# A two-layer hybrid transformer block on one core: the last layer's z modulations left out, and the low parts of the last branch and the output projection moved to VectorE

## The chip, the cores and the metric

The kernel runs on one core of a Trainium2 chip. The metric is the device time of one execution in microseconds (us); the medians given are over repeated executions. The engines are named as in the profile: PE is TensorE (matmuls; PEld its weight loads), DVE is VectorE, ACT is ScalarE, POOL is GpSimd, SP is SyncE, which here issues most DMAs.

## The reference

Two token streams, x (512 tokens) and z (256 context tokens) of width 1024, go through two layers. The modulations of a layer are six vectors of 1024 for x and six for z. In the last layer (`need_ctx` false) z is only read by the token mixers: its outputs, and so all of its modulations past the first two, are used by nobody.

```python
def hybrid_layer(x, z, c, c_ctx, p, rope_ret, rope_mla, need_ctx):
    mod_x = jax.nn.silu(c) @ p['w_ada'] + p['b_ada']
    mod_z = jax.nn.silu(c_ctx) @ p['w_ada'] + p['b_ada']
    sh1x, sc1x, g1x, sh2x, sc2x, g2x = [m[:, None, :] for m in jnp.split(mod_x, 6, axis=-1)]
    sh1z, sc1z, g1z, sh2z, sc2z, g2z = jnp.split(mod_z, 6, axis=-1)
    hx = x * (1.0 + sc1x) + sh1x
    hz = z * (1.0 + sc1z) + sh1z
    mix_x, mix_z = token_mixers(hx, hz, p, rope_ret, rope_mla, need_ctx)
    x = layer_norm(DEEPNORM_ALPHA * x + g1x * mix_x, p['ln_gain'][0], p['ln_bias'][0])
    x = layer_norm(DEEPNORM_ALPHA * x + g2x * sq_relu_mlp(x * (1.0 + sc2x) + sh2x, p),
                   p['ln_gain'][1], p['ln_bias'][1])
    if need_ctx:
        ...
    else:
        z = None
    return x, z
```

`token_mixers` sums three gated branches, `sigmoid(gate) * (y @ w_branch)`, and multiplies the sum by `w_out` (the output projection). `sq_relu_mlp` is `square(relu(h @ w_ff1)) @ w_ff2`.

## The kernel before

**Products in three matmuls.** All activations lie feature-major, 128 features by tokens. A float32 operand is kept as a pair: a high part (`hi_of`, ScalarE, a rounding copy to fp32r) and a low part (`lo_of`, source minus high part). Line 386 is every such subtraction; it runs on VectorE unless another engine is given. A product is three matmuls (lines 432 to 434): weight high by operand high, weight high by operand low, weight low by operand high. So line 433 waits for the operand's low part and line 434 for the weight's.

**Weights.** `weight` loads a 128x1024 block (tile `wraw`, three buffers), makes the high part on ScalarE and the low part in two halves: the first `w_dve` columns on VectorE, the others on GpSimd. `W_DVE` is 512. The pair goes to one of three buffers `wsp`, which TensorE frees; three blocks of the last layer's output projection (`KEPT`, tile `w`) have buffers of their own.

**Modulations.** Each layer has 48 units of 128 features. A unit is one 512 KB load and, per stream, one 128x1024 multiply-and-reduce on VectorE (line 500, tile `cond`), then a small adjustment of both results (line 506). Units 0 to 15 are shift and scale of the first half-layer. Layer 0's units from 16 on and all 48 of layer 1 are made during layer 0 by `modulations`, a generator that the rest of the program advances at set rates (`later.step`) and empties after round 6 of the MLP (`later.rest`). After the first 24 its loads have one buffer only, `graw`: the next load starts when the unit's last reduction is done.

**Branches.** `branch` computes for each of 8 feature tiles f, and for each stream, a matmul group into a PSUM bank (`pd`, three buffers; `pst` for two early ones), then VectorE multiplies it by the gate (line 1492, tile `ms`, gate tile `gl`) and the product is added to the total (line 1493, tile `t`). In the last branch (`final`) the addition is on VectorE and the total is split into `op`, the operand of the output projection: high part on ScalarE, low part on GpSimd. A bank is free again after line 1492. Layer 0 has both streams (512 and 256 columns), layer 1 only x.

**Output projection and MLP.** Per tile f of the projection, one weight block and 24 matmuls, then line 1719 (residual) and the sums for the layer norm (lines 1507 to 1513). The MLP has 8 rounds j: `ff1` (relu on ScalarE, square on VectorE, line 1756, tile `rl`, split into `op`), then `ff2`, whose banks VectorE drains into the accumulators (line 1770; in round 6 followed by line 1772, which uses a gate modulation; in round 7 line 1774). Rounds 0 and 7 go stream by stream, rounds 1 to 6 take both.

**Order.** A scheduler orders each engine's instructions when the program is built, by the order of the code and its own estimates; `keep_in_program_order` pins the reductions of `modulations` among themselves. Each engine then runs its list strictly in order.

Of the kernel before, what the change touches and what calls it, by code (L numbers as in the profile page):

```python
# [16 lines left out]
DEPTH = 2  # L17
# [21 lines left out]
W_DVE = 512  # L39

KEPT = (2, 3, 4)
# [271 lines left out]
def block_kernel(ctx, tc, xT, zT, cond, wu, sp, bias, tab, out):  # L313
# [65 lines left out]
    act, dve, pool, pe, sync = nc.scalar, nc.vector, nc.gpsimd, nc.tensor, nc.sync  # L379
# [19 lines left out]
    for l in range(DEPTH):  # L399
        t = const.tile([128, SP_N], F32, name=f"sp{l}")  # L400
# [16 lines left out]
    def weight(*key, own=False, spare=False, w_dve=W_DVE):  # L417
        raw = load(*key, spare=spare)
        if own:
            w = (dbl("w"), dbl("w"))  # L420
        else:
            t = wsp.tile([128, 2, 1024], F32, tag="wsp", name=nm("wsp"))
            w = (t[:, 0], t[:, 1])
        hi_of(w[0], raw)
        for eng, cols in ((dve, slice(0, w_dve)), (pool, slice(w_dve, 1024))):
            if cols.start < cols.stop:
                lo_of(w[1][:, cols], raw[:, cols], w[0][:, cols], eng)
        return w
# [26 lines left out]
    mods = [const.tile([128, 48, 2], F32, name=f"mod{l}") for l in range(DEPTH)]  # L455
# [34 lines left out]
    def modulation(l, c, raw, cs, pinned=False, shared=()):  # L490

        for t in shared:
            h = dbl("prod")
            pool.tensor_tensor(h, raw, cs[t], op=ALU.mult)
            act.activation(h, h, AF.Copy, scale=0.5, accum_out=mods[l][:, c, t : t + 1])
            dve.tensor_scalar(mods[l][:, c, t : t + 1], mods[l][:, c, t : t + 1], spt[l][:, SP_BADA + c : SP_BADA + c + 1], 0.0, op0=ALU.add, op1=ALU.add)
        for t in [t for t in range(2) if t not in shared]:
            i = dve.tensor_tensor_reduce(cs[2], raw, cs[t], 0.5, spt[l][:, SP_BADA + c : SP_BADA + c + 1], ALU.mult, ALU.add, mods[l][:, c, t : t + 1])  # L500
            if pinned:
                tc.keep_in_program_order(i)
        m = mods[l][:, c, :]
        add, mul = MOD_ADJUST[c // 8]
        if (add, mul) != (0, 1):
            dve.tensor_scalar(m, m, float(add), float(mul), op0=ALU.add, op1=ALU.mult)
# [70 lines left out]
    def split_into(pair, src, eng=None):  # L577
        hi_of(pair[0], src)
        lo_of(pair[1], src, pair[0], eng)
# [870 lines left out]
    def branch(l, b, sizes, ops, gates, total, final, midway=None):  # L1450

        fresh = not total
        if fresh:
            total.extend(new_tiles(n, KT) for n in sizes)
        tiles = [(f, g, n) for f in range(KT) for g, n in enumerate(sizes)]

        def fetch(f, g, n):
            t = ft("gl")[:, :n]  # L1460
            sync.dma_start(t, gates[b, f][g])
            return t

        ahead = fetch(*tiles[0])
        early = []
        ops = [[o[g] for o in ops] for g in range(len(sizes))]
        for i, (f, g, n) in enumerate(tiles):
            if midway and i == len(tiles) // 2:
                midway()
            if f % 2 == 0 and g == 0:  # L1470
                w = weight(l, "br", b, f // 2)
                if final and f == 0:

                    for ff, gg, nn in tiles[: 2 * len(sizes)]:
                        ps = (bank_d() if gg == 0 else bank_t())[:, :nn]
                        fm(ps, w, 512 * ff, ops[gg], range(3), 4)
                        early.append(ps)
            t = ahead
            if i + 1 < len(tiles):
                ahead = fetch(*tiles[i + 1])  # L1480
            if early:
                ps = early.pop(0)
                fm(ps, w, 512 * (f % 2), ops[g], [3], 4)
            else:
                ps = bank_d()[:, :n]
                fm(ps, w, 512 * (f % 2), ops[g], range(4), 4)
            a = total[g][f]
            if fresh:
                dve.scalar_tensor_tensor(a, t, 1.0, ps, ALU.add, ALU.mult)
            else:  # L1490
                s = sgl("ms")[:, :n]
                dve.scalar_tensor_tensor(s, t, 1.0, ps, ALU.add, ALU.mult)  # L1492
                (dve if final else pool).tensor_tensor(a, a, s, op=ALU.add)
                if final:
                    split_into(final[g][f], a, pool)
            yield cost(12 * n)


# [126 lines left out]
    for l in range(DEPTH):  # L1625
        need = l < DEPTH - 1
# [74 lines left out]
        def out_weight(f):  # L1701

            if f in kept:
                return kept.pop(f)
            w = weight(l, "out", f, own=not need and r == 0 and f in KEPT)
            if not need and r == 0 and f in KEPT:
                kept[f] = w
            return w

        later.until(1 + 8)  # L1710
        for r, (b, cols) in enumerate(rounds):
# [20 lines left out]
            for f in range(f0, KT):  # L1732
                w = out_weight(f)
# [11 lines left out]
        for j in range(8):  # L1745
            apart = j in (0, 7)
            for rnd in [[r] for r in rounds] if apart else [[(b, slice(0, n)) for b, (_, n) in enumerate(bufs)]]:
# [3 lines left out]
                for i in range(4):  # L1751
                    w = weight(l, "ff1", j, i)
                    for g, ps in enumerate(fm_groups(w, 0, hs, KT)):
                        t = sgl("rl")[:, : ns[g]]
# [22 lines left out]
                for i in range(4):  # L1777
                    w = weight(l, "ff2", j, i)
# [90 lines left out]
```

## Time and profile before

| | |
|---|---|
| median of 3 runs | 2669.43 us (2669.32 to 2672.81) |
| profiled execution | 2672.0 us, span 2670.0 us |
| PE busy | 2524.7 us, 95% of the span |
| DVE busy | 1801.6 us, 67% |
| ACT busy | 1157.5 us, 43% |
| POOL busy | 1048.8 us, 39% |
| mean granted clock of TensorE | 0.978 |

The profiled execution is 2.0 us longer than its span, and 2.6 us above the median. A busy share is an average over stages with different limits; for the change, the stages to look at are the last branch and output projection of layer 0 (about 870 to 960 us), rounds 1 to 7 of layer 0's MLP (about 1060 to 1540 us), and the last branch and output projection of layer 1 (about 2200 to 2290 us).

### The profile page before, as it was taken

How to read it: one execution, taken by the hardware profiler on the slowest of the kernel's cores; microseconds unless marked ns; L12 is line 12 of the kernel's file. 1: busy time of each engine (PE TensorE's matmuls, PEld its weight loads, DVE VectorE, ACT ScalarE, POOL GpSimd, SP SyncE). 2: the span in 40 equal slices, each digit the busy share in tenths (PEclk: the TensorE clock that was granted, in tenths of full speed). 3: DMA queues.
4: the chain of work that ended last, by engine and by line, in shares of the span. 5: the costliest groups of instructions: out<-in, count | busy, mean ns of one | idle time of the engine just before them, and what ended most of it. 6: DMA issues, size and time to landing. Idle time of an engine off the chain costs nothing. (4 is left out here: it accounts for less than half of the span.)

```text
span 2670.0 us, 40740 instructions
## 1 busy us (share of the span) xinstructions
PE 2524.7 (95%) x15218; PEld 2241.1 (84%) x15218; DVE 1801.6 (67%) x3326; ACT 1157.5 (43%) x2176; POOL 1048.8 (39%) x816
## 2 busy tenths in 40 slices
PE   6999999997999898999999989999999899999997
PEld 4899998987888787888888878888888788888887
DVE  8565556676978894767777775566568758734357
ACT  4555545563323345222222345555556434632225
POOL 6312113345335655222222452222334557743334
PEclk8999999999999999999999999999999999999999
DMA  6222223423665543344444423332342356433333
GB/s 237 72 87 83 72 85 95 141 78 98 237 205 153 191 127 103 111 133 125 134 134 122 133 83 114 96 96 88 117 149 91 103 185 206 127 111 95 98 100 119
DMA packets 143001, 329.48 MB, mean 123 GB/s; under 512 B 16978, under 2 KB 54738, under 8 KB 142804
## 3 DMA queue, kind: packets, MB, share of 16 engines
q1 hardware_dynamic: 132436, 311.15, 37.7%
q10 hardware_dynamic: 10368, 15.73, 1.6%
q8 instruction: 120, 1.97, 0.3%
q14 instruction: 77, 0.63, 0.1%
HBM read 288.27 MB, written 36.45 MB: 122 GB/s over the span
## 5 line engine op out<-in xcount | busy, mean ns | idle before, releaser
L432 PE MATMUL pd<-op,wsp 128*128 128x512 f32 (+1 forms) x3080 | 1074.8, 350 | 38.6 <-DVE ms L1492 8.4
L433 PE MATMUL pd<-op,wsp 128*128 128x512 f32 (+1 forms) x3080 | 1073.0, 348 | 14.6 <-DVE op L386 8.4
L434 PE MATMUL pd<-op,wsp 128*128 128x512 f32 (+1 forms) x3080 | 1069.3, 347 | 7.1 <-DVE wsp L386 7.1
L386 POOL TENSOR_TENSOR wsp<-wraw,wsp 128x512 fp32r<-128x512 f32 x317 | 522.3, 1650 | 988.3 <-ACT wsp L383 874.3
L432 PEld LDWEIGHTS pd<-op,wsp 128*128 128x128 f32 x3080 | 588.6, 192 | 115.8 <-ACT op L588 10.0
L433 PEld LDWEIGHTS pd<-op,wsp 128*128 128x128 f32 x3080 | 590.2, 192 | 87.7 <-DVE op L386 12.3
L434 PEld LDWEIGHTS pd<-op,wsp 128*128 128x128 f32 x3080 | 589.3, 191 | 80.1 <-DVE wsp L386 9.4
L383 ACT ACTIVATE wsp<-wraw 128x1024 fp32r<-128x1024 f32 x319 | 336.2, 1055 | 391.5 <-PE pd L434 271.1
L386 DVE TENSOR_TENSOR wsp<-wraw,wsp 128x512 fp32r<-128x512 f32 (+1 forms) x319 | 283.3, 889 | 190.7 <-ACT wsp L383 184.7
L647 PE MATMUL pd<-wsp,op 128*128 128x256 f32 x704 | 203.1, 289 | 2.5 <-DVE pr L757 2.0
L649 PE MATMUL pd<-wsp,op 128*128 128x256 f32 x704 | 201.3, 286 | 0.2 <-POOL wsp L386 0.2
L648 PE MATMUL pd<-wsp,op 128*128 128x256 f32 x704 | 201.1, 286 | 0.0
L500 DVE CUSTOM_DVE_ANT_0 cond<-graw,cond,sp 128x1024 bf16<-128x1024 f32 x112 | 167.5, 1495 | 43.3 <-DMA graw<-wu 42.8
L1756 DVE TENSOR_TENSOR rl<-rl 128x256 f32<-128x256 f32 (+1 forms) x104 | 68.6, 659 | 138.9 <-ACT rl L1755 138.6
L386 DVE TENSOR_TENSOR pt<-pst,pt 128x512 fp32r<-128x512 f32 (+1 forms) x208 | 121.3, 602 | 48.2 <-ACT pt L383 46.4
L647 PEld LDWEIGHTS pd<-wsp,op 128*128 128x128 f32 x704 | 137.1, 195 | 3.6 <-issue 2.8
L649 PEld LDWEIGHTS pd<-wsp,op 128*128 128x128 f32 x704 | 136.6, 194 | 0.8 <-POOL wsp L386 0.4
L648 PEld LDWEIGHTS pd<-wsp,op 128*128 128x128 f32 x704 | 137.0, 195 | 0.1
L1770 DVE TENSOR_TENSOR t<-pd,t 128x512 f32<-128x512 f32 (+1 forms) x132 | 80.4, 613 | 77.6 <-PE pd L434 77.4
L1755 ACT ACTIVATE rl<-pd 128x256 f32<-128x256 f32 (+1 forms) x104 | 51.6, 496 | 174.3 <-PE pd L434 174.2
L616 PE MATMUL pso<-pt,t 128*128 128x256 f32 x704 | 115.3, 293 | 10.7 <-DVE ntx L623 4.0
L383 ACT ACTIVATE pt<-pst 128x512 fp32r<-128x512 f32 (+1 forms) x208 | 104.8, 529 | 46.4 <-PE pst L599 39.8
(284 smaller groups left out, 3925.8 us busy)
## 6 DMA issues: line engine op xcount, KB each, us to landing
wraw<-wu SPq DMA_DIRECT2D x327, 512.0 KB, 3.7
graw<-wu SPq DMA_DIRECT2D x56, 512.0 KB, 3.7
ada<-wu SPq DMA_DIRECT2D x40, 512.0 KB, 5.7
gg<-gate ACTq DMA_DIRECT2D x48, 256.0 KB, 2.0
gl<-gg SPq DMA_DIRECT2D x48, 256.0 KB, 3.6
zbias<-bias SPq DMA_DIRECT2D x64, 128.0 KB, 2.3
t<-vd SPq DMA_DIRECT2D x28, 256.0 KB, 5.4
gd<-gt SPq DMA_DIRECT2D x40, 128.0 KB, 2.4
```

What stands on the lines that cost most here:

```text
L383: act.activation(R(dst), src, AF.Copy, scale=scale)
L386: (eng or dve).tensor_tensor(R(dst), src, hi, op=ALU.subtract)
L432: pe.matmul(ps, R(a[0]), R(b[0]), start=start, stop=False)
L433: pe.matmul(ps, R(a[0]), R(b[1]), start=False, stop=False)
L434: pe.matmul(ps, R(a[1]), R(b[0]), start=False, stop=stop)
L500: i = dve.tensor_tensor_reduce(cs[2], raw, cs[t], 0.5, spt[l][:, SP_BADA + c : SP_BADA + c + 1], ALU.mult, ALU.add, mods[l][:, c, t : t + 1])
L616: pe.matmul(o, R(vts[k]), R(pts[k]), start=k == 0, stop=k == n - 1)
L647: pe.matmul(ps, R(a[0]), R(w[0][:, o : o + 256]), start=k == 0, stop=False)
L648: pe.matmul(ps, R(a[1]), R(w[0][:, o : o + 256]), start=False, stop=False)
L649: pe.matmul(ps, R(a[0]), R(w[1][:, o : o + 256]), start=False, stop=k == nk - 1)
L1756: dve.tensor_tensor(t, t, t, op=ALU.mult)
L1770: dve.tensor_tensor(a, ps, a, op=ALU.add)
```

## The change

1. In the last layer, units 16 to 47 make only the modulation of x; the reduction for z is left out, and the adjustment of line 506 covers one column. The loads are as they were. These 32 units are the last that `modulations` makes.
2. The weights of the last branch and of the output projection, in both layers, take their low part whole on VectorE (`w_dve` 1024): one subtraction of 1024 columns in place of one of 512 there and one of 512 on GpSimd.
3. The low part of the last branch's total is made on VectorE, not on GpSimd.

```diff
-        for t in [t for t in range(2) if t not in shared]:
+        for t in [t for t in range(2) if t not in shared and (t == 0 or c < 16 or l < DEPTH - 1)]:
             i = dve.tensor_tensor_reduce(cs[2], raw, cs[t], 0.5, spt[l][:, SP_BADA + c : SP_BADA + c + 1], ALU.mult, ALU.add, mods[l][:, c, t : t + 1])
             if pinned:
                 tc.keep_in_program_order(i)
-        m = mods[l][:, c, :]
+        m = mods[l][:, c, : 2 if c < 16 or l < DEPTH - 1 else 1]
...
-                w = weight(l, "br", b, f // 2)
+                w = weight(l, "br", b, f // 2, w_dve=1024 if final else W_DVE)
...
                 if final:
-                    split_into(final[g][f], a, pool)
+                    split_into(final[g][f], a)
...
-            w = weight(l, "out", f, own=not need and r == 0 and f in KEPT)
+            w = weight(l, "out", f, own=not need and r == 0 and f in KEPT, w_dve=1024)
```

The diff does not show where the scheduler puts the instructions. The matmuls of TensorE stand in the same order as before. Three places on VectorE matter.

VectorE at the start of round 6's `ff2` in layer 0, before: `cond` is a reduction's output, `graw` its load, `t` from `pst` or `pd` a drain.

```order
L386 TENSOR_TENSOR op_14356<-rl_14636,op_14356 128x512
L500 ISA cond_7004,mod_104<-graw_14573,cond_7004,sp_95 128x1024
L500 ISA mod_104 128x1
L500 ISA cond_7004,mod_104<-graw_14573,cond_7005,sp_95 128x1024
L500 ISA mod_104 128x1
L506 TENSOR_SCALAR mod_104<-mod_104 128x2
L1770 TENSOR_TENSOR t_10891<-pst_14652,t_10891 128x256
L1772 SCALAR_TENSOR_TENSOR t_10891<-t_10891,mod_103,t_9837 128x256
L1770 TENSOR_TENSOR t_10893<-pd_14662,t_10893 128x512
```

The same place in the changed kernel:

```order
L386 TENSOR_TENSOR op_14314<-rl_14590,op_14314 128x512
L500 ISA cond_7004,mod_104<-graw_14527,cond_7004,sp_95 128x1024
L500 ISA mod_104 128x1
L506 TENSOR_SCALAR mod_104<-mod_104 128x1
L1770 TENSOR_TENSOR t_10871<-pst_14605,t_10871 128x256
L1772 SCALAR_TENSOR_TENSOR t_10871<-t_10871,mod_103,t_9837 128x256
L1770 TENSOR_TENSOR t_10873<-pd_14615,t_10873 128x512
```

One reduction instead of two stands ahead of the first drains; the rest is in place.

VectorE at the last modulations, in `ff1` of round 7 (z), before; `rl` is a square, `wsp` a weight's low part.

```order
L500 ISA cond_7004,mod_104<-graw_14857,cond_7005,sp_95 128x1024
L500 ISA mod_104 128x1
L1756 TENSOR_TENSOR rl_14966<-rl_14966 128x256
L506 TENSOR_SCALAR mod_104<-mod_104 128x2
L386 TENSOR_TENSOR wsp_15045<-wraw_15043,wsp_15045 128x512
L1756 TENSOR_TENSOR rl_15002<-rl_15002 128x256
L386 TENSOR_TENSOR wsp_15083<-wraw_15081,wsp_15083 128x512
L500 ISA cond_7004,mod_104<-graw_14928,cond_7004,sp_95 128x1024
L500 ISA mod_104 128x1
L1756 TENSOR_TENSOR rl_15038<-rl_15038 128x256
L500 ISA cond_7004,mod_104<-graw_14928,cond_7005,sp_95 128x1024
L500 ISA mod_104 128x1
```

In the changed kernel:

```order
L506 TENSOR_SCALAR mod_104<-mod_104 128x1
L1756 TENSOR_TENSOR rl_14914<-rl_14914 128x256
L386 TENSOR_TENSOR wsp_14993<-wraw_14991,wsp_14993 128x512
L500 ISA cond_7004,mod_104<-graw_14877,cond_7004,sp_95 128x1024
L500 ISA mod_104 128x1
L1756 TENSOR_TENSOR rl_14950<-rl_14950 128x256
L506 TENSOR_SCALAR mod_104<-mod_104 128x1
L386 TENSOR_TENSOR wsp_15031<-wraw_15029,wsp_15031 128x512
L1756 TENSOR_TENSOR rl_14986<-rl_14986 128x256
L386 TENSOR_TENSOR wsp_15070<-wraw_15068,wsp_15070 128x512
L386 TENSOR_TENSOR op_14882<-rl_14986,op_14882 128x256
```

The last reduction has moved from between the second and the fourth square to ahead of the second.

VectorE in the last branch of layer 0, at a pair of layer 0's own modulations (load `ada_8682`), before; the third row is the line-1492 product of the third z tile.

```order
L500 ISA cond_7004,mod_103<-ada_8682,cond_7004,sp_93 128x1024
L500 ISA mod_103 128x1
L1492 SCALAR_TENSOR_TENSOR ms_9993<-gl_9953,pd_9980 128x256
L500 ISA cond_7004,mod_103<-ada_8682,cond_7005,sp_93 128x1024
L500 ISA mod_103 128x1
L1493 TENSOR_TENSOR t_8781<-t_8781,ms_9993 128x256
L506 TENSOR_SCALAR mod_103<-mod_103 128x2
L1492 SCALAR_TENSOR_TENSOR ms_10013<-gl_9978,pd_10000 128x512
```

In the changed kernel, with the new low parts `op`:

```order
L1492 SCALAR_TENSOR_TENSOR ms_9991<-gl_9951,pd_9978 128x256
L386 TENSOR_TENSOR op_9827<-t_8778,op_9827 128x512
L500 ISA cond_7004,mod_103<-ada_8682,cond_7004,sp_93 128x1024
L500 ISA mod_103 128x1
L1493 TENSOR_TENSOR t_8781<-t_8781,ms_9991 128x256
L500 ISA cond_7004,mod_103<-ada_8682,cond_7005,sp_93 128x1024
L500 ISA mod_103 128x1
L386 TENSOR_TENSOR op_9834<-t_8781,op_9834 128x256
L506 TENSOR_SCALAR mod_103<-mod_103 128x2
L1492 SCALAR_TENSOR_TENSOR ms_10011<-gl_9976,pd_9998 128x512
```

The product that drains the third z tile now stands ahead of both reductions; the one of the fourth x tile still stands behind them.

## Rows read from the trace of the kernel before

**Rows 1.** The page, part 1: busy us (share), instructions.

```profile
PE 2524.7 (95%) x15218; PEld 2241.1 (84%) x15218; DVE 1801.6 (67%) x3326; ACT 1157.5 (43%) x2176; POOL 1048.8 (39%) x816
```

**Rows 2.** Busy time by stretch: stretch, us, PE PEld DVE ACT POOL, PEclk, DMA, GB/s.

```profile
873.00:915.00 42.00, 38.02 (x217) 32.87 (x216) 32.16 (x44) 12.09 (x20) 26.27 (x22) 0.96 0.64 217
...
893.90:897.30 3.40, 3.40 (x10) 2.65 (x9) 3.40 (x8) 1.94 (x3) 1.68 (x2) 0.50 0.39 132
...
1457.10:1460.50 3.40, 3.40 (x11) 2.72 (x10) 3.40 (x8) 0.00 (x0) 0.00 (x0) 0.50 0.03 7
...
1498.10:1504.90 6.80, 5.88 (x28) 5.65 (x27) 4.09 (x8) 2.50 (x5) 2.93 (x3) 0.50 0.59 199
...
2217.00:2240.00 23.00, 21.81 (x110) 18.55 (x111) 19.82 (x22) 10.19 (x14) 20.12 (x13) 1.00 0.73 250
```

**Rows 3.** Timeline of PE, 1250 to 1505: start, us, operation [idle before <-releaser].

```profile
1264.11 0.38 PE L432 MATMUL pd<-op,wsp 128*128 128x256 f32 x1 [0.54 <-DVE t L1770]
...
1455.83 0.50 PE L432 MATMUL pd<-op,wsp 128*128 128x512 f32 x1 [1.99 <-DVE t L1770]
...
1495.61 0.38 PE L432 MATMUL pd<-op,wsp 128*128 128x256 f32 x1 [2.04 <-ACT op L383]
...
1496.70 0.38 PE L433 MATMUL pd<-op,wsp 128*128 128x256 f32 x1 [0.71 <-DVE op L386]
...
1499.25 0.58 PE L432 MATMUL pd<-op,wsp 128*128 128x256 f32 x1 [0.92 <-ACT op L383]
```

**Rows 4.** Summary of the reductions of line 500, 1252 to 1497: ns min/median/max, idle.

```profile
L500 DVE CUSTOM_DVE_ANT_0 cond<-graw,cond,sp x64: 1268/1283/2401, 1252.8 to 1495.0; 128x1024 bf16<-128x1024 f32 x64
...
  DMA graw<-wu: 26.4, 18
```

**Rows 5.** Timeline of DVE ahead of the wait that ends at 1455.83.

```profile
1450.59 1.29 DVE L500 CUSTOM_DVE_ANT_0 cond<-graw,cond,sp 128x1024 bf16<-128x1024 f32 x1 [0.56 <-DMA graw<-wu]
...
1451.92 1.28 DVE L500 CUSTOM_DVE_ANT_0 cond<-graw,cond,sp 128x1024 bf16<-128x1024 f32 x1
...
1455.10 0.68 DVE L1770 TENSOR_TENSOR t<-pd,t 128x512 f32<-128x512 f32 x1
```

**Rows 6.** Timeline of DVE ahead of the wait that ends at 1495.61.

```profile
1482.77 2.32 DVE L500 CUSTOM_DVE_ANT_0 cond<-graw,cond,sp 128x1024 bf16<-128x1024 f32 x1
...
1485.62 2.40 DVE L500 CUSTOM_DVE_ANT_0 cond<-graw,cond,sp 128x1024 bf16<-128x1024 f32 x1
...
1492.14 1.55 DVE L500 CUSTOM_DVE_ANT_0 cond<-graw,cond,sp 128x1024 bf16<-128x1024 f32 x1 [1.39 <-DMA graw<-wu]
...
1493.63 1.47 DVE L1756 TENSOR_TENSOR rl<-rl 128x256 f32<-128x256 f32 x1
```

**Rows 7.** Timeline of DVE, then of PE, in the last branch of layer 0.

```profile
890.51 1.81 DVE L500 CUSTOM_DVE_ANT_0 cond<-ada,cond,sp 128x1024 bf16<-128x1024 f32 x1
...
892.25 0.41 DVE L1492 SCALAR_TENSOR_TENSOR ms<-gl,pd 128x256 f32<-128x256 f32 x1
...
892.81 0.47 PE L432 MATMUL pd<-op,wsp 128*128 128x512 f32 x1 [2.46 <-DVE ms L1492]
```

**Rows 8.** Timeline of PE in the output projections of layers 0 and 1.

```profile
922.76 0.39 PE L434 MATMUL pd<-op,wsp 128*128 128x256 f32 x1 [1.40 <-DVE wsp L386]
...
927.10 0.39 PE L434 MATMUL pd<-op,wsp 128*128 128x256 f32 x1 [1.20 <-DVE wsp L386]
...
2238.25 0.39 PE L433 MATMUL pd<-op,wsp 128*128 128x256 f32 x1 [0.59 <-POOL op L386]
```

**Rows 9.** Groups of DVE by shape, whole span: count | busy us, mean ns | idle before.

```profile
L386 DVE TENSOR_TENSOR pt<-pst,pt 128x256 fp32r<-128x256 f32 x64 | 26.4, 412 | 0.0
...
L386 DVE TENSOR_TENSOR wsp<-wraw,wsp 128x1024 fp32r<-128x1024 f32 x2 | 2.4, 1220 | 3.2 <-ACT wsp L383 3.2
```

**Rows 10.** Groups of DVE by shape in the stretch 873 to 915.

```profile
L386 DVE TENSOR_TENSOR wsp<-wraw,wsp 128x512 fp32r<-128x512 f32 x5 | 8.2, 1633 | 0.3 <-ACT wsp L383 0.3
L1493 DVE TENSOR_TENSOR t<-t,ms 128x512 f32<-128x512 f32 x8 | 6.9, 862 | 0.1
L1493 DVE TENSOR_TENSOR t<-t,ms 128x256 f32<-128x256 f32 x8 | 6.6, 825 | 0.1
```

**Rows 11.** The same groups in the last branch of layer 1, 2217 to 2240.

```profile
L1493 DVE TENSOR_TENSOR t<-t,ms 128x512 f32<-128x512 f32 x8 | 8.2, 1039 | 0.3
```

## The prediction

> **What bounds the kernel now.** The reading goes from the page's busy shares to busy time by stretch, then to PE's timeline with the engine that ended each idle time, and from there to that engine's own timeline. The page has PE at 95% and DVE at 67% [rows 1]. So only idle time and slow clock of PE can be won, about 145 us in all, and DVE work counts only where PE waits for it. The order of PE's matmuls is not changed by the edit; what can change is when their operands and banks are ready.
>
> Three stretches carry PE waits that hang on work the edit touches.
>
> *Rounds 1 to 7 of layer 0's MLP.* While VectorE makes the last 64 reductions (32 units, two streams, half of them now unwanted), PE waits five times for something that stands behind a reduction on VectorE: .54, 1.99, 2.04, .71 and .92 us [rows 3], together 6.2. [...]
>
> The wait that ends at 1455.83 comes from two reductions of 1.29 and 1.28 us that stand ahead of the drains, after .56 us in which VectorE waits for their load [rows 5]. The one that ends at 1495.61 comes from two reductions of 2.32 and 2.40 us, whose end at 1488.0 lets the next load start; the next reduction begins at 1492.14 after 1.39 us of waiting for that load, and the third square `rl` only at 1493.63 [rows 6]. Elsewhere in these rounds most of the 64 reductions (median 1.28 us, 26.4 us of idle ahead of 18 of them [rows 4]) sit under PE's matmuls and cost nothing.
>
> *Last branch and output projection of layer 0.* PE waits 2.46 us at 892.81 for a z tile's product that stands behind a reduction of 1.81 us [rows 7], and the clock is .50 for 3.4 us after it [rows 2]. In the projection it waits 1.40 and 1.20 us for the VectorE half of a weight's low part [rows 8].
>
> *Last branch of layer 1.* PE waits .59 us for the last low part of the total, which GpSimd makes [rows 8].
>
> **Part 1, the reductions.** Thirty-two reductions go: 32 x 1.28 = 41 us of VectorE at the median [rows 4]. Their cover is PE, so only the five waits and two falls of the clock count. At 1455.83 the second reduction goes (1.28), and the load, which has one buffer and starts when the unit before is done, starts a reduction earlier, so that the .56 of waiting goes too: 1.84 of 1.99. I take 1.7; what is late next is the drain itself, .68 [rows 5], which stays. At 1495.61 the load starts after the single reduction, about 1485.1 in place of 1488.0; from 1488.0 to 1492.1 it took 4.1, so its reduction can start at about 1489.2 and now stands ahead of the second square, not the third. The third square, 3 us earlier, is there before PE wants it at 1493.6. Of 2.04 + .71 + .92 = 3.7 I take 3.2, since splits on ScalarE and VectorE remain behind each square. The .54 at 1264.11 goes nearly whole, .5. With a wait short, the clock should not fall: 5.1. Sum 1.7 + 3.2 + .5 + 5.1 = **10.5**, between 5.4 (the clock falls all the same) and 11.3.
>
> **Parts 2 and 3, the low parts.** No row shows VectorE making low parts of the total. The same operation on 256 columns takes .41 and on 1024 columns 1.22 [rows 9], which puts 512 at .68. That is the lower bound; the upper one is what VectorE's operations take while GpSimd works: weights' halves of 512 columns have a mean of 1.63, additions of 256 columns .83 [rows 10]. I take the short values, because in these two stretches GpSimd's operations (22 and 13 [rows 2]) are, but for one or two, the very low parts that leave.
>
> Layer 0's last branch: added 8 x .68 + 8 x .41 = 8.7. A weight's whole low part at 1.22 replaces a half at 1.63: 5 x .41 = 2.1 saved. Additions come down from .86 to .68 and from .83 to .41: 8 x .18 + 8 x .42 = 4.8 saved; two reductions from 1.81 to 1.28: 1.1. Net +.7 on 32.2 busy of 42 us [rows 2]: VectorE stays below PE. Layer 1's last branch: added 8 x .68 = 5.4; saved 4 x .41 on weights and 8 x .36 on additions of 1.04 [rows 11] = 4.5. Net +.9 on 19.8 of 23 us [rows 2]; tight, not full.
>
> What PE gets: the product that ended the 2.46 us now stands ahead of both reductions, so I leave .5 of that wait: 2.0 gained. The fourth x tile's product still stands behind them, now with two more low parts in between: a new wait, bounded by 0 and by the old 2.46; I take 1.5, two reductions at 1.28 and the low part of .41 less the slack of one tile. Net .5, and the lower clock goes with the long wait, 1.7 (bounds 0 and 1.7). Of the two waits in the projection (2.6) one goes, since VectorE comes there with less behind it; the other stays, because a 1024 piece takes .54 longer than a 512 one: 1.3. The .59 of layer 1 goes, because .68 on VectorE is shorter than GpSimd's mean of 1.55 there (20.1 us in 13 operations [rows 2]): .6. Sum .5 + 1.7 + 1.3 + .6 = **4.1**, between -1.5 (nothing won, the new wait whole) and 7.4 (all these waits and the clock, no new wait).
>
> ScalarE's and SyncE's lists move by a load or two; I cost that at nothing, under 5% DMA share around the first stretch [rows 2], at most one wait for a load of some 1.4 us [rows 6].
>
> **Sum.** 10.5 + 4.1 = 14.6. The profiled execution (2672.0, 2.0 of it outside its span) lies 2.6 above the median of 2669.43; the waits are not a share of that, so it is taken off either: 2657.4 for a profile like this one, 2669.4 - 14.6 = **2655** for the median.
>
> **Rivals.**
>
> *The low parts buy nothing.* A matmul group needs the first columns of the weight's low part first. Before, VectorE's half was there .68 after the high part; one piece of 1024 is there after 1.22. If that decides, the projection's waits become .54 longer each, the new wait eats the 2.46, and the clock falls at 893.9 as before: parts 2 and 3 come to between 0 and -1.5 - 2 x .54 = -2.6, and the time to 2669.4 - 10.5 = 2658.9, at most 2661.5. For it: VectorE stands behind `wsp` in both waits [rows 8]. Against: these halves took 1.63 there, not .68 [rows 10]. 22%.
> [...]
>
> *The reductions buy nothing.* The load has one buffer and SyncE issues it in its own strict order. If an earlier entry of SyncE's list holds it, the load does not start earlier, VectorE waits for it as 18 times before [rows 4], and a square or drain behind it is as late as ever. Then only the 4.1 stay: 2665.3. Against: the load of 1492.1 lands 4.1 us after the last reduction's end [rows 6], so it looks as if that end, and no other entry, released it. 10%.
>
> *Slower: VectorE becomes the bound of the last branches.* This happens if something other than GpSimd, such as the loads at 217 to 250 GB/s [rows 2], stretches VectorE's operations. Then nothing is saved, and the added work is at least 11.4 + 7.6 = 19.0 (layer 0: 8.7 + 5 x .54; layer 1: 5.4 + 4 x .54), at most 27.8 + 19.6 = 47.4 (at 1.63 and .83 each). VectorE has 9.8 + 3.2 = 13.0 idle there [rows 2]; the rest lands on the path. Halfway, 33.2 - 13.0 = 20.2, less the 10.5: 9.7 slower, 2679. It decides from 23.5 us of added work on, a sixth of the way. For it: layer 1 has 3.2 us to spare. Against: the same shapes take .41 and .68 where GpSimd is still. 6%.
>
> *It does not show.* Every fall of the clock comes back at another wait, and waits move to the next drain: under 5 us, some 2666 to 2669. 7%.
>
> **How the numbers follow.** Forecast 50%; its own range goes from one fall of the clock left in each part (10.5 - 1.7 and 4.1 - 1.7: 11.2 saved) to the upper bounds (11.3 + 7.4 = 18.7), which is 2650.7 to 2658.2. More than that, where the shorter queues also take small waits that I did not count: 5%, down to 2647. With the rivals' 22, 10, 6 and 7 that is 100. The range 2647 to 2665.5 leaves out the slower case, the last rival and a little of the others, some 15%. A measurement tells 0.2%, 5.3 us, from no change. Faster by more: 50 + 5 + 22 = 77%; within: 10 + 7 = 17%; slower: 6%.
>
> **What would show it.** In the profile after, line 500 has 32 `graw` reductions between 1250 and 1490; PE starts round 6's `ff2` and round 7's z squares with waits under .8, and the clock rows there read 1.00. If the waits are gone and the clock is still .50, the 5.1 was mis-sized. In the last branches the additions should read .68 and .41, the new low parts the same; means above 1 us speak for the slower case. At the third z tile's place PE should wait about .5, at the next one about 1.5. If PE waits for `wsp` at more blocks of the projection than two, the first rival holds. The forecast is wrong if the total of PE's idle time before 1250 rises, or if idle time of the MLP's rounds falls by less than 3 us.

## The result

The changed kernel takes 2652.19 us (median of 6 runs, 2651.02 to 2656.53) beside 2669.82 us for the kernel before on the same chip: a ratio of 0.9934, 95% interval 0.9921 to 0.9947, 17.6 us faster. A second comparison gave 0.9936 (0.9922 to 0.9949). The forecast was 2655, the range 2647 to 2665.5.

The page of the changed kernel, part 1 (busy us, share, instructions), answers to [rows 1]:

```profile
PE 2518.4 (95%) x15218; PEld 2238.0 (84%) x15218; DVE 1759.0 (66%) x3286; ACT 1158.3 (44%) x2176; POOL 966.1 (36%) x755
```

VectorE lost 43 us and GpSimd 83 us of busy time, and the span only 18.9: most of both engines' work lay under TensorE's. Both profiles hold 15218 matmuls in the same order, so the n-th of one can be set against the n-th of the other. The start of a matmul after, less its start before, is called its drift here; where the drift steps, time was won or lost. Places are given as the time of the matmul in the kernel before. In the pair of profiles the drift steps by -6.2 us between 840 and 960 (last branch and projection of layer 0), by -1.2 up to 1112, -0.7 at 1264, -3.5 at 1455 to 1460, -4.3 at 1495 to 1504, -1.8 at 1627 to 1631 (layer 1's start), 0 in the last branch of layer 1, and -1.3 at 2270 (the layer norm behind it).

Busy time by stretch in the changed kernel answers to [rows 2] (stretch; PE, PEld, DVE, ACT, POOL; granted clock, DMA share, GB/s). The middle rows cover the places where the clock was at 0.50:

```profile
873.00:915.00 42.00, 39.52 (x244) 34.98 (x243) 33.49 (x62) 11.97 (x20) 1.64 (x1) 1.00 0.69 225
...
889.00:895.00 6.00, 3.99 (x21) 3.15 (x21) 5.97 (x14) 1.93 (x4) 0.00 (x0) 1.00 0.47 155
1446.00:1452.00 6.00, 6.00 (x34) 5.21 (x34) 5.96 (x13) 0.00 (x0) 1.29 (x1) 1.00 0.31 87
1486.00:1494.00 8.00, 8.00 (x67) 7.77 (x66) 6.20 (x12) 3.61 (x7) 4.55 (x4) 1.00 0.52 168
2200.00:2223.00 23.00, 21.80 (x112) 18.73 (x113) 20.32 (x29) 9.41 (x13) 0.60 (x1) 1.00 0.73 255
```

The clock stays at 1.00 in all of them. VectorE is hardly fuller than before: 33.5 us in the branch of layer 0 (32.2 before), 20.3 in that of layer 1 (19.8), while GpSimd falls from 26.3 to 1.6 and from 20.1 to 0.6.

VectorE's groups by shape in 873 to 915 (count, busy us, mean ns) answer to [rows 10]:

```profile
L386 DVE TENSOR_TENSOR wsp<-wraw,wsp 128x1024 fp32r<-128x1024 f32 x5 | 6.1, 1218 | 0.0
L386 DVE TENSOR_TENSOR op<-t,op 128x512 fp32r<-128x512 f32 x8 | 5.5, 684 | 0.0
L1493 DVE TENSOR_TENSOR t<-t,ms 128x512 f32<-128x512 f32 x8 | 5.5, 682 | 0.0
...
L386 DVE TENSOR_TENSOR op<-t,op 128x256 fp32r<-128x256 f32 x8 | 3.4, 419 | 0.6 <-ACT op L383 0.5
L1493 DVE TENSOR_TENSOR t<-t,ms 128x256 f32<-128x256 f32 x8 | 3.3, 417 | 0.0
```

The new low parts (`op`) add 8.9 us. The additions fell from 862 and 825 ns to 682 and 417, which saves 4.7 of them, and the weights' subtractions from 8.2 to 6.1 us, which saves 2.1 more. The rest is about what the shorter reductions save (2026 to 1280 ns on the mean).

What is left of TensorE's waits (its timeline, [idle before <-releaser]), to set beside [rows 3, 7, 8]:

```profile
889.65 0.47 PE L432 MATMUL pd<-op,wsp 128*128 128x512 f32 x1 [0.60 <-DVE ms L1492]
894.03 0.38 PE L432 MATMUL pd<-op,wsp 128*128 128x256 f32 x1 [1.41 <-DVE ms L1492]
...
919.11 0.39 PE L434 MATMUL pd<-op,wsp 128*128 128x256 f32 x1 [1.28 <-DVE wsp L386]
951.85 0.65 PE L730 MATMUL pss<-ctab,tiny 128*128 128x128 f32 x4 [1.03 <-POOL tiny L1526]
...
1483.85 0.39 PE L433 MATMUL pd<-op,wsp 128*128 128x256 f32 x1 [1.41 <-DVE op L386]
...
2201.20 0.50 PE L433 MATMUL pd<-op,wsp 128*128 128x512 f32 x1 [1.30 <-DVE op L386]
```

The 2.46 is 0.60, and the new wait stands at the next tile with 1.41. One of the two waits for `wsp` is left. The waits at 1264 and 1455 are gone. Of the three at 1495 to 1499 one of 1.41 is left, at line 433, and 0.31 at the third. The 1.41 no longer stands behind a reduction: it ends with the subtraction `op` that starts at 1482.31 and takes 1.48 us, while GpSimd makes two pieces of weights (1481.75 to 1484.94); in the kernel before the same subtraction, with GpSimd still, took 0.41.

### The profile page after: what moved, and what is told of

Same layout as the page of the kernel before. It is cut to its first block, busy times and chain, and to the rows that moved or that the text cites. A ratio compares the mean times of both kernels' runs of the same rounds, so it can differ in the third digit from the quotient of the medians.

```text
span 2651.1 us, 40614 instructions
## 1 busy us (share of the span) xinstructions
PE 2518.4 (95%) x15218; PEld 2238.0 (84%) x15218; DVE 1759.0 (66%) x3286; ACT 1158.3 (44%) x2176; POOL 966.1 (36%) x755
## 5 line engine op out<-in xcount | busy, mean ns | idle before, releaser
L386 POOL TENSOR_TENSOR wsp<-wraw,wsp 128x512 fp32r<-128x512 f32 x283 | 473.9, 1677 | 957.9 <-ACT wsp L383 847.7
L386 DVE TENSOR_TENSOR wsp<-wraw,wsp 128x512 fp32r<-128x512 f32 (+1 forms) x319 | 293.2, 920 | 191.7 <-ACT wsp L383 190.3
L1756 DVE TENSOR_TENSOR rl<-rl 128x256 f32<-128x256 f32 (+1 forms) x104 | 76.1, 732 | 160.0 <-ACT rl L1755 159.8
L500 DVE CUSTOM_DVE_ANT_0 cond<-graw,cond,sp 128x1024 bf16<-128x1024 f32 x80 | 119.5, 1493 | 26.1 <-DMA graw<-wu 26.0
```

Of the source, the lines that this page charges most:

```text
L386: (eng or dve).tensor_tensor(R(dst), src, hi, op=ALU.subtract)
L1756: dve.tensor_tensor(t, t, t, op=ALU.mult)
```

## The experiments

Every kernel here keeps the order of TensorE's matmuls. Times are medians. A run's time stands beside that of the kernel before in the same comparison, and the gain in us is what the ratio makes of that median, which was 2667.0 for the first four, 2671.1 for the next four, 2670.1 for the next three and 2673.1 for the last.

### Part 1 alone, and parts 2 and 3 alone

`e1_reductions` has only the first two hunks of the diff, `e2_low_parts` only the other three.

> Part 1 alone: the 32 reductions of z go, all low parts stay where they were. Theory (only PE's waits and the clock falls behind them count, and the two traces put 0.7 us at the wait of 1264, 3.5 around 1455 to 1460 and 4.4 around 1495 to 1504): 8.6 us faster, 2661.2. Rival (the load's single buffer holds the reduction as late as ever, and the gain of the full change there came from the low parts): less than 2 us faster, 2668 or more. In the profile the waits at 1264, 1455 and 1495 and the two falls of the clock are gone, those at 892, 922 and 927 stay.

> Parts 2 and 3 alone: the low parts of the last branch, of its weights and of the output projection on VectorE, all 64 reductions kept. Theory: the gain between 880 and 970 us (6.8 by the two traces) and 1.3 at layer 1's layer norm, together 8.1: 2661.7. Rival (the low parts buy nothing; what moved there is the accident of one execution): within 2 us of before, 2668 to 2670. The waits at 1455 and 1495 stay as before.

Part 1 alone: 2659.59 us, ratio 0.9967 (0.9955 to 0.9978), 8.8 us. Parts 2 and 3 alone: 2657.82, ratio 0.9964 (0.9946 to 0.9982), 9.6 us. Both rivals fall: the intervals leave 5.9 to 12.0 us to the one and 4.8 to 14.4 to the other. The two add up to 18.4, about the whole. TensorE's timeline in part 1 alone, then in parts 2 and 3 alone:

```profile
891.65 0.47 PE L432 MATMUL pd<-op,wsp 128*128 128x512 f32 x1 [2.46 <-DVE ms L1492]
...
1488.83 0.39 PE L433 MATMUL pd<-op,wsp 128*128 128x256 f32 x1 [1.42 <-DVE op L386]
```

```profile
895.39 0.39 PE L432 MATMUL pd<-op,wsp 128*128 128x256 f32 x1 [1.38 <-DVE ms L1492]
...
1448.66 0.50 PE L432 MATMUL pd<-op,wsp 128*128 128x512 f32 x1 [0.75 <-DVE t L1770]
...
1487.26 0.39 PE L432 MATMUL pd<-op,wsp 128*128 128x256 f32 x1 [2.43 <-ACT op L383]
```

Each part moves its own places: part 1 leaves 2.46 in the branch, and 1.42 in round 7 as in the full change; parts 2 and 3 leave 2.43 in round 7. The 0.75 was not expected: all reductions are there. VectorE's timeline shows why. The first fence is the second profile of the kernel before (below), the second parts 2 and 3 alone:

```profile
1447.52 1.28 DVE L500 CUSTOM_DVE_ANT_0 cond<-graw,cond,sp 128x1024 bf16<-128x1024 f32 x1 [1.38 <-DMA graw<-wu]
...
1450.18 1.10 DVE L506 TENSOR_SCALAR mod<-mod 128x2 f32<-128x2 f32 x1
```

```profile
1444.33 1.29 DVE L500 CUSTOM_DVE_ANT_0 cond<-graw,cond,sp 128x1024 bf16<-128x1024 f32 x1 [0.46 <-DMA graw<-wu]
...
1446.99 0.17 DVE L506 TENSOR_SCALAR mod<-mod 128x2 f32<-128x2 f32 x1
```

The load lands 0.5 or 1.4 us late, and between the pair and the drains the same small instruction takes 0.17 or 1.10 us. GpSimd's timeline in the second profile of before has the reason for the latter:

```profile
1449.43 1.82 POOL L386 TENSOR_TENSOR wsp<-wraw,wsp 128x512 fp32r<-128x512 f32 x1 [6.57 <-ACT wsp L383]
```

GpSimd's piece of a weight ends at 1451.25, and line 506, begun inside it, at 1451.28. In the two kernels with one of parts 2 and 3 (below) it is 1.10 again and ends 0.03 us behind such a piece; in the first profile of before the piece starts later, and line 1772 takes 1.40 in place of 0.48. In parts 2 and 3 alone the piece starts only at 1447.70, behind line 506. So this wait has no fixed size: it hangs on the load and on where GpSimd's piece falls. That in parts 2 and 3 alone, with 3 us won at 1455 to 1460, it is theirs and not that execution's is not shown.

### Which of the 32 reductions count

```
e3_last_eight:  ... not in shared and (t == 0 or l < DEPTH - 1 or not (c >= 40))]
e4_first_24:    ... not in shared and (t == 0 or l < DEPTH - 1 or not (16 <= c < 40))]
```

> The reductions of z are left out in units 40 to 47 of layer 1 only (8 of 32, the last ones, from about 1436 us on). Theory (two places count): 3.5 + 4.4 = 7.9 faster, 2661.9. Rival (VectorE's relief of 41 us counts as a whole, whatever the place): a quarter of 8.6, 2.2 faster, 2667.6.

> The reductions of z are left out in units 16 to 39 only (24 of 32), and kept in the last eight. Theory: 0.7 us faster at most, 2669.1, although VectorE loses 31 us of work. Rival (the relief as a whole): three quarters of 8.6, 6.5 faster, 2663.3.

The last eight: 2660.32, ratio 0.9975 (0.9961 to 0.9989), 6.7 us, near the 7.9 expected. The first 24: 2661.28, ratio 0.9972 (0.9960 to 0.9985), 7.5 us, where I expected 0.7; the rival named 6.5. But they are not shares of one relief, since 8 and 24 of 32 give the same. The profile of the first 24 shows both the pair of reductions ahead of round 6's drains and TensorE without any wait over 0.4 there; what is left is round 7's:

```profile
1444.92 1.27 DVE L500 CUSTOM_DVE_ANT_0 cond<-graw,cond,sp 128x1024 bf16<-128x1024 f32 x1
...
1446.23 1.28 DVE L500 CUSTOM_DVE_ANT_0 cond<-graw,cond,sp 128x1024 bf16<-128x1024 f32 x1
```

```profile
1488.72 0.38 PE L432 MATMUL pd<-op,wsp 128*128 128x256 f32 x1 [2.04 <-ACT op L383]
1489.82 0.39 PE L433 MATMUL pd<-op,wsp 128*128 128x256 f32 x1 [0.71 <-DVE op L386]
```

The pair no longer waits for its load (0.56 in [rows 5]) and starts, against the matmuls, 2.6 us earlier than in the kernel before: with one reduction a unit, the one-buffer chain of loads had run ahead, and this load is issued 4.4 us earlier. So the wait at 1455 has two remedies, one reduction less or an earlier load, and both experiments win it. Only round 7's wait needs the last reductions to go. My theory was wrong in taking a place for a count of reductions; the places themselves hold.

### Parts 2 and 3 apart

`e5_weights` has only `w_dve=1024` (both lines), `e6_totals` only `split_into(final[g][f], a)`.

> Part 2 alone: the weights of the last branch and of the output projection take their low part whole on VectorE; the totals' low parts stay on GpSimd, and all reductions stay. Theory (the waits for wsp in the projection and for GpSimd in the two layer norms are what these pieces cost): 2.0 at 927, 0.7 at 957, 1.3 at 2270, together 4 us faster, 2663 against 2667 for the kernel before; the wait of 2.46 at 892 stays above 2, since sixteen low parts still run on GpSimd in the branch. Rival (whole pieces finish later): the waits for wsp in the projection become longer, no gain, 2666 to 2668.

> Part 3 alone: the low parts of the last branch's total are made on VectorE, the weights' second halves stay on GpSimd, and all reductions stay. Theory (GpSimd's sixteen operations are what stretches VectorE in the branch, and their place in its list moves a drain ahead of the reductions): 1.0 at 883, 0.8 at 888, 1.9 and a fall of the clock at 892, less a new wait of 1.4: 3 to 4 us faster, about 2663.5. VectorE's additions in the branch take 0.68 and 0.42, and 0.7 to 0.9 only where a weight's half runs on GpSimd. Rival (VectorE is full in the branch): waits of more than 1 us at three or more feature tiles, no gain or slower, 2667 or more.

The weights alone: 2665.21, ratio 0.9977 (0.9967 to 0.9987), 6.1 us. The totals alone: 2670.22, ratio 0.9999 (0.9989 to 1.0009): nothing, which the theory had not expected. It is the rival's time, but not its picture, for only two tiles of the branch wait about 1 us or more (0.98 and 2.50). The totals alone, TensorE's timeline, then VectorE's and GpSimd's at the same place:

```profile
887.35 0.47 PE L432 MATMUL pd<-op,wsp 128*128 128x512 f32 x1 [0.61 <-DVE ms L1492]
892.82 0.38 PE L432 MATMUL pd<-op,wsp 128*128 128x256 f32 x1 [2.50 <-DVE ms L1492]
...
924.06 0.58 PE L434 MATMUL pd<-op,wsp 128*128 128x256 f32 x1 [2.43 <-DVE wsp L386]
```

```profile
889.05 1.50 DVE L1493 TENSOR_TENSOR t<-t,ms 128x256 f32<-128x256 f32 x1
```

```profile
888.23 2.04 POOL L386 TENSOR_TENSOR wsp<-wraw,wsp 128x512 fp32r<-128x512 f32 x1 [9.31 <-ACT wsp L383]
```

The wait of 2.46 went to the next tile whole, and in the projection 0.26 and 2.43 stand where 1.40 and 1.20 stood; the clock falls behind both long waits (256-column matmuls come 0.21 us apart there, 0.12 once it is back). GpSimd's one piece of a weight there stretches the addition between the two reductions from 0.42 to 1.50, and that 1.08 is the difference between the 2.50 here and the 1.41 of the full change. At this place the totals need the weights: with these moved too, only one operation of GpSimd's is left in the branch (x1 in the table above). The weights alone leave the 2.45 in the branch (at 892.48) and have 0.52 and 1.22 in the projection, at the matmuls of 917 and 923, in place of 1.40 and 1.20 at those of 923 and 927. The times alone don't show that the two edits together gain more than their sum: 6.1 and 0.3 lie within the interval of both together (4.8 to 14.4).

### The kernels before and after once more

> The kernel before, for a second profile. Theory (the waits stand in the lists and come in every execution; which of them the clock answers with a fall differs): waits near 883, 892, 922, 927, 1455 and 1495 of the same size within 0.5 us, the falls of the clock at 893, 1457 and 1498 at least in part. Rival (the waits at 1455 and 892 were an accident of one execution): they are absent, and about 5 us of the forecast gain was no gain of the change. Time 2667, ratio 1.000.

> The changed kernel, for a second profile and more runs beside the same runs of before. Theory: ratio 0.9934 within its interval, 17 us; the waits at 883 to 892, 1455 and 1495 are as small as in its first profile and the one new wait of 1.4 at the fourth x tile stands. Rival (a part of the 17 us was an accident of the executions compared): ratio 0.995 or above.

The kernel before repeated at 2670.32 (ratio 1.0002, 0.9994 to 1.0011), the changed one at 2653.54 (0.9936). In the second profile of before:

```profile
891.76 0.47 PE L432 MATMUL pd<-op,wsp 128*128 128x512 f32 x1 [2.46 <-DVE ms L1492]
...
1452.78 0.62 PE L432 MATMUL pd<-op,wsp 128*128 128x512 f32 x1 [3.14 <-DVE t L1770]
1494.46 0.58 PE L433 MATMUL pd<-op,wsp 128*128 128x256 f32 x1 [2.79 <-DVE op L386]
```

The waits of the branch and the projection come again (2.46, 1.40 and 1.21). Those of the MLP are not the same within 0.5 us, as the theory had it: 2.79 and 0.23 stand where 2.04, 0.71 and 0.92 stood, and the wait at 1455 was 1.99 in the first profile, 3.14 here, 3.02 and 3.08 in the two kernels with one of parts 2 and 3. The clock fell in the three places again, each time for 3.4 us. The second profile of after has the same 1.40 and 1.42 left, and no fall at the three places.

### Breaking the whole pieces up

```diff
-        for eng, cols in ((dve, slice(0, w_dve)), (pool, slice(w_dve, 1024))):
+        parts = ... if w_dve < 1024 else ((dve, slice(0, 512)), (dve, slice(512, 1024)))
+        for eng, cols in parts:
```

> The changed kernel, with each of the 25 whole low parts (1024 columns, 1.22 us) made in two VectorE pieces of 512. First theory (one whole piece makes TensorE wait 0.54 longer where it waits for the first columns at all): the wait of 1.28 in the projection shrinks to about 0.7, VectorE has 25 x 0.14 = 3.5 us more to do under cover; 0.5 to 1 us faster than the changed kernel, 2652. [...] Second rival (the extra piece pushes the products behind it back): slower by 1 us or more, 2654.5.

2653.39 us, ratio 0.9934 (0.9922 to 0.9946): the time of the changed kernel. TensorE's timeline:

```profile
893.52 0.53 PE L433 MATMUL pd<-op,wsp 128*128 128x256 f32 x1 [1.86 <-DVE ms L1493]
...
919.61 0.39 PE L435 MATMUL pd<-op,wsp 128*128 128x256 f32 x1 [0.75 <-DVE wsp L386]
```

The wait for the weight shrinks from 1.28 to 0.75, by the 0.54 of the first theory, and that of 1.03 at the layer norm is gone. But the wait in the branch, behind one piece more, grows from 1.41 to 1.86, and in this profile the clock falls behind it (at 893.6, 3.4 us): in drift 2.0 lost there, 1.7 won at the other two.

### GpSimd busy again, and its control

```diff
                     split_into(final[g][f], a)
+                    for o in range(0, n - 200, 224):
+                        pool.tensor_tensor(scr.tile([128, 224], BF16, ...), a[:, o : o + 224], final[g][f][0][:, o : o + 224], op=ALU.subtract)
```

> The changed kernel, with GpSimd made to subtract again in the last branches: beside VectorE's low part it computes 224 or 2 x 224 columns of the same difference into a buffer that nobody reads (24 tiles, 40 operations). Theory (GpSimd's work beside VectorE's is what stretches VectorE): additions and low parts in the branch of layer 0 rise from 0.68 and 0.42 to 0.8 to 1.1 on the mean, the wait of 1.4 at the fourth x tile grows by about 1, a fall of the clock near 893 may come back: 2 to 4 us slower than the changed kernel, 2655 to 2657. Rival (VectorE's stretching came from transfers or from something else): the means stay at 0.68 and 0.42 and the time at 2653.

2656.63 us, ratio 0.9946 (0.9934 to 0.9958), 3 us slower than the changed kernel. VectorE's groups in 873 to 915, then TensorE's timeline:

```profile
L387 DVE TENSOR_TENSOR op<-t,op 128x512 fp32r<-128x512 f32 x8 | 8.3, 1042 | 0.0
L1494 DVE TENSOR_TENSOR t<-t,ms 128x512 f32<-128x512 f32 x8 | 6.4, 798 | 0.0
L387 DVE TENSOR_TENSOR op<-t,op 128x256 fp32r<-128x256 f32 x8 | 6.1, 768 | 0.5 <-ACT op L384 0.5
...
L1494 DVE TENSOR_TENSOR t<-t,ms 128x256 f32<-128x256 f32 x8 | 5.2, 651 | 0.0
```

```profile
880.96 0.39 PE L433 MATMUL pd<-op,wsp 128*128 128x256 f32 x1 [1.95 <-DVE ms L1493]
884.22 0.47 PE L433 MATMUL pd<-op,wsp 128*128 128x512 f32 x1 [1.57 <-DVE ms L1493]
889.95 0.58 PE L433 MATMUL pd<-op,wsp 128*128 128x256 f32 x1 [2.73 <-DVE ms L1493]
```

VectorE's additions and low parts take 0.65 to 1.04 where they took 0.42 and 0.68, and GpSimd has 24 operations of 1.02 us on the mean beside them (one operation in the changed kernel), so its work is the cause. The products of line 1492 (1493 here), which read one of their two inputs from PSUM, take 0.41 and 0.68 as before. The drift against the changed kernel rises by 10.7 us between that kernel's 884 and 922, with two falls of the clock (behind the matmuls of 889.95 and 919.53 the 256-column ones come 0.21 us apart in place of 0.12), and by 4.3 in the last branch of layer 1. The whole kernel lost only 3, because this one ran ahead by 9.8 us before 840, where no operation was added: the 448-byte buffer stands in front of the weights' buffers and shifts them and those behind them. The last experiment is the control: the rates of the next one, that buffer, and one subtraction.

### Moving what is left, and the shifted buffers

```diff
-ADA_BRANCH = 0.05
-ADA_MLP = 1.1
+ADA_BRANCH = 0.0
+ADA_MLP = 1.25
```

> The changed kernel with two rates altered: no modulation is made in the last branch (rate 0.05 to 0), and those of the MLP are made faster (1.1 to 1.25 a step), so that the pair of reductions leaves the branch and the last one ends before round 7. Theory (what is left of the two places is the wait of 1.4 behind the pair and 1.4 behind the last reduction): both waits go, 2.5 to 3 us faster than the changed kernel, 2650. Rival (they move again: more reductions stand in the rounds of the MLP and in the projection): a new wait of 1 us or more at an earlier drain or at the projection, 2653 or slower.

> The kernel of e9_units_moved with the 448-byte buffer of e8_gpsimd_busy in front of the weights' buffers and one subtraction into it in place of forty: the control for that run. There, outside the two last branches, TensorE ran ahead of the changed kernel by 9.8 us up to 840 us, with 188 ns for most weight loads where it has 192, and 113 to 118 ns from one 256-column matmul to the next where it has 120. Theory (the shifted addresses of the weights cause this): the weight loads are at 188 again, about 10 us faster than e9_units_moved, 2638 to 2640. Rival (it came from that execution or chip): 192 and 120 ns again, 2649. In the first case GpSimd's work in that run cost about 13 us, not the 3 that its time shows.

With the rates: 2648.85 us, ratio 0.9925 (0.9910 to 0.9939), about 4 us below the changed kernel by the medians, though the intervals overlap. The wait in the branch is gone (-1.2 in drift). In round 7 a wait of 0.92 is left with no reduction ahead of it, so the last reduction was not all that made it: here too `op` takes 1.50 beside a piece of GpSimd's. The larger part came where no gain was expected, at rounds 1 and 2. The changed kernel, then this one:

```profile
1105.38 0.50 PE L432 MATMUL pd<-op,wsp 128*128 128x512 f32 x1 [2.63 <-DVE t L1770]
...
1176.87 0.50 PE L432 MATMUL pd<-op,wsp 128*128 128x512 f32 x1 [2.81 <-DVE t L1770]
```

```profile
1104.28 0.50 PE L432 MATMUL pd<-op,wsp 128*128 128x512 f32 x1 [1.65 <-DVE t L1770]
...
1173.05 0.50 PE L432 MATMUL pd<-op,wsp 128*128 128x512 f32 x1 [1.69 <-DVE t L1770]
```

Each wait is 1 us shorter and neither is followed by a fall of the clock (in the changed kernel some 3.4 us at 0.50 at each): -5.3 in drift, against +3.0 given back between 920 and 1000 of the changed kernel. The next run, with the same rates, has 1.59 and 1.70 there. But short waits at these matmuls came without the rates too: 0.22 and 1.70 in the profile of the last eight, where nothing ahead of them was edited, and 1.67 at the second in the second profile of before. The other 21 of 24 are 2.5 to 3.0. So the rates probably shorten them; that all of the -5.3 is theirs is not shown.

With the shifted buffers as well: 2644.52 us, ratio 0.9901 (0.9884 to 0.9917), clear of the changed kernel's 0.9936 (0.9922 to 0.9949) and the fastest run here. Its interval overlaps that of the rates alone. TensorE's weight loads between 120 and 500 us (count, busy us, mean ns), the rates alone and then with the shift:

```profile
L648 PEld LDWEIGHTS pd<-wsp,op 128*128 128x128 f32 x244 | 46.7, 192 | 0.0
```

```profile
L649 PEld LDWEIGHTS pd<-wsp,op 128*128 128x128 f32 x248 | 46.7, 188 | 0.0
```

The shift comes with loads of 188 ns again, so it was not one execution. Its size was missed: not 10 us but 4.3 by the medians, 6.4 by the ratios, and 5.7 by the drift between the two profiles at 840. So about 4 to 6 of the 9.8 us lead are the shift, and the rest of that lead stays open (1.8 of it came in the first 100 us, where the profiles differ by as much without it); GpSimd's work in the run before cost more than the 3 us that its time shows, some 7 to 9.

## Why the prediction was right

The forecast was 14.6 us, the measured gain 17.6. Step by step:

**Part 1: 10.5 forecast, 8.8 measured alone.** At 1455 the drift gave 3.5, the forecast wait and clock 1.7 + 1.7. At 1495 it gave 4.3 where 3.2 + 3.4 stood. That term was too large on both counts. The waits gave 2.1: 1.41 stays at line 433 (0.5 in all was left in the sum), against the sign that waits there would be under 0.8, because the forecast had no term for GpSimd's pieces beside VectorE in round 7. The clock gave 2.2. The forecast's 5.1 for the two falls, 1.7 and 3.4, is half of the 3.4 and 6.8 us at 0.50 in [rows 2]; that half of such time is lost was the author's estimate, and no run shows it: half of the 6.8 us counted time in which TensorE waited ([rows 2] has 5.88 busy there), and its 256-column matmuls came 0.21 us apart there and 0.12 behind it, which is less than half lost. The mechanism at 1455 was named in its right parts (one reduction, and an earlier load), but the load proved enough by itself.

**Parts 2 and 3: 4.1 forecast, 9.6 measured alone.** In layer 0's branch the steps hold one by one: 0.5 forecast and 0.60 found at the old place, 1.5 and 1.41 at the new one, 1.7 and 1.3 for the clock, prices of 0.68 and 0.41 against 0.684 and 0.419, one of two waits for `wsp` left. What the sum lacked were waits that were not in it: the 0.69 at 883 goes, the projection gives 2.0 (0.4, 0.2 and 1.4 at the matmuls of 917, 923 and 927) where 1.3 stood, and the matmuls of the two layer norms, which wait for `tiny`, start 0.7 and 1.3 us earlier. At the layer norm of layer 0, TensorE, VectorE and GpSimd before, then VectorE after:

```profile
957.54 0.65 PE L730 MATMUL pss<-ctab,tiny 128*128 128x128 f32 x4 [1.61 <-POOL tiny L1526]
951.72 1.27 DVE L1535 TENSOR_TENSOR tiny<-sp,mod 128x8 f32<-128x8 f32 x1
951.66 1.30 POOL L386 TENSOR_TENSOR wsp<-wraw,wsp 128x512 fp32r<-128x512 f32 x1
```

```profile
946.61 0.15 DVE L1535 TENSOR_TENSOR tiny<-sp,mod 128x8 f32<-128x8 f32 x1
```

Line 1535 stands ahead of the last VectorE step for `tiny` in VectorE's list. This operation on 8 columns took as long as GpSimd's half of a weight and now takes 0.15: 1.12 less, of which the longer weight piece behind it takes 0.54 back. The layer norm of layer 1 had the same (1.26, now 0.15). GpSimd itself was idle ahead of its own step for `tiny` (2.80 us in layer 0).

In layer 1's last branch, where 0.6 was forecast, the 0.59 went, but in this pair the wait of 0.67 at 2217 became 1.30 and nothing was won. In the second profiles of both kernels neither has a wait at that matmul, and 0.8 was won. Besides, the run of these parts alone holds 3 us at 1455 that I cannot give to them. The 9.6 lies above the upper bound of 7.4, though its interval reaches down to 4.8. The lower bound of -1.5 has the new wait at 1.5 and not whole, as it says; whole, at 2.46, it would be -2.5.

**The rivals.** That the low parts buy nothing, and that the reductions buy nothing, fell with the two runs of each alone. Against TensorE's matmuls the load of round 6's last reduction is issued 6.0 us earlier in the changed kernel and the last load of all 2.9 us earlier, the 1485.1 in place of 1488.0 of the forecast: the end of the reduction did release it. That VectorE becomes the bound fell on its condition: the stretching goes with GpSimd (additions of 0.68 and 0.42 us with one operation of GpSimd's in the branch, of 0.80 and 0.65 with 24). The run with GpSimd busy shows what stretching costs, 10.7 us in one branch and the start of its projection.

**What it did not see.** The forecast took each wait from one profile as its size. The wait at 1455 runs from 0.75 to 3.14 us in the five profiles that have all 64 reductions. And 1.8 us at the start of layer 1, where nothing was edited, are in the pair of profiles by a fall of the clock (1627.8, 3.4 us at 0.50) that only one of them has. That fall comes again in the second profile of before, and at this place in none of the other twelve, not even in that of the totals alone, which gained nothing; whether the change removes it is open. The 145 us that the forecast says can be won are TensorE's idle time alone; what the lower clock costs lies within its busy time (3.40 of 3.40 us at 0.50, from 893.9 and from 1457.1). Errors of 2 to 5 us in single terms had opposite signs: that the total was nearer than its terms is in part luck.

## What to carry to other kernels

Work taken off an engine that is not the bound is worth only what a bound engine waits for behind it, so cost it place by place, and allow that a place may be cured by an earlier load as well as by less work. An edit that leaves the disturbance of another in place can be worth nothing alone: here the totals gained 0 without the weights. When VectorE looks slow beside GpSimd, take GpSimd's work out of the stretch as a whole before deciding that VectorE has no room, and look at its smallest operations too, for they may stand on the path (line 1535 here, with 1.27 us beside GpSimd's piece and 0.15 without).

## What the runs showed of the hardware

- VectorE's operations took longer where GpSimd ran a subtraction beside them: a 128x256 addition (line 1493) 1.50 us beside one of 2.04, 0.42 without; a 128x8 operation (line 1535) 1.27 beside one of 1.30, 0.15 without; a 128x2 operation with one input (line 506) 1.10 beside one of 1.82, 0.17 without. The products of line 1492, with one input in a PSUM bank, kept 0.41 and 0.68 in the run with GpSimd busy.
- At the two matmuls shown at 1105 and 1176, behind waits of 2.63 and 2.81 us, the changed kernel's granted clock was 0.50 for some 3.4 us. In the fourteen profiles such a fall stands behind 20 of the 21 waits of 2.5 to 3.0 us at these matmuls (none behind 2.89 at 1106 in the second profile of the changed kernel), and behind none of the seven of 0.22 to 1.70. At 893 it is less regular: after 2.45 us the fall was absent in two kernels (the first 24 reductions, the weights alone), and after 1.86 it came in one (the two pieces).
- A shift of the weights' buffers, and those behind them, by 448 bytes a partition went with weight loads of 188 ns in place of 192, and 4.3 us of the whole by the medians. Why is open.
